# Down projection of a hybrid decoder block: from eight block products to seven

## Chip, core and metric

The kernel runs on one core of a Trainium2 chip. The metric is device time in microseconds (us): the median of several executions of the whole kernel, from launch to the last output byte. Beside it there is one profiled execution, whose trace gives every duration quoted below.

## The reference

One decoder layer on 512 tokens of width 1024, all in float32: a normalised three-branch token mixer with a residual, a normalised convolutional feed-forward part with a residual, and a last RMSNorm. The change touches what follows the up projection:

```python
def conv_ffn(h, w_up, conv_w, conv_b, w_down):          # FFN_DIM = 2816
    up = h @ w_up                                        # 512 x 5632
    up = lax.conv_general_dilated(up, ...) + conv_b      # causal, width 3, per channel
    gate, val = jnp.split(up, 2, axis=-1)
    return (jax.nn.silu(gate) * val) @ w_down            # (512 x 2816) @ (2816 x 1024)
...
    x = x + conv_ffn(rmsnorm(x, norm_ffn), w_up, conv_w, conv_b, w_down)
return rmsnorm(x, norm_final)
```

## The kernel before

**Arithmetic.** A float32 factor is split into a high half (a copy in a TensorE format, `copy_act`, made by ScalarE) and a low half (the value less the high half, made by VectorE). A product is then three matmuls, high x high, high x low and low x high (`mm3m`, L176 to L179). Activations (`gh`, `gl`) are the stationary operand of the down projection, weights (`whi`, `wlo`) the moving one.

**Stages.** After the mixer come the up projection (`up_unit`, 11 chunks c, each with two gate and two value strips of 128 channels), and the down projection (`down_unit`). Each strip of the gated product is `cc[:, 2 + a, :]`, 128 channels x 512 tokens; L1122 and the lines behind it make `gh` and `gl` of it, one stage behind TensorE. The down projection makes four token tiles of 128 in two column halves of 512, each over 22 strips: 4 x 2 x 22 x 3 matmuls of 512 columns. The last tile's last four strips are cut into 256-column pieces (`fin`), so that its result comes in two parts.

**Weights.** A `Chunk` is loaded by one DMA from SyncE's queue into one of two raw buffers of 1 MB (`Chunk.load`, L81), and split piece by piece (`Chunk.split`, L92 is the low half) into the four `whi` and four `wlo` buffers of 128 x 1024.

**Order.** All instructions are written out in a fixed order by `run`: for each unit, first the splits that are due, then functions that `before` or `early` have planned, then the unit's matmuls. Every engine works its own list in that order and waits for semaphores. SyncE's queue is in order too, so a load that waits for a buffer holds up those behind it.

**End.** The residual `x1` stays in SBUF. Each result is added to it by VectorE, squared and summed by ScalarE (L1193), raised to -1/2 by GpSimd (L1211), scaled, and stored by eight DMAs (`finish`).

Of the kernel before, what the change touches and what calls it, by code (L numbers as in the profile page):

```python
# [9 lines left out]
F32 = mybir.dt.float32  # L10
# [8 lines left out]
T = 512  # L19
# [12 lines left out]
def hybrid_block(  # L32
# [19 lines left out]
    def slot(shape, dt=F32, name="s"):  # L52
        return sl.tile(shape, dt, tag="s", name=name)
# [100 lines left out]
    def krows(w, k0, nk, c0, mk=None):  # L154
# [45 lines left out]
    def run(first, live):  # L200
# [9 lines left out]

        def load_to(n):
            while state["loaded"] < min(n, len(order)):
                order[state["loaded"]].load()
# [897 lines left out]
    gh, gl, cc = {}, {}, []  # L1111
    fps = {}

    def up_use(c, a, val):
        ps = fps.pop((c, a, val))
        if not cc:
            cc.append(y8([128, 4, T], name="cc"))
        f = 2 * c + a
        g, v = cc[0][:, a, :], cc[0][:, 2 + a, :]
        if not val:  # L1120
            conv(g, ps, f)
            later.append(lambda: S.activation(g, g, AF.Silu))  # L1122
            return
# [8 lines left out]
        later.append(product)  # L1132

    def up_unit(chunk, c, a, val, o, tag):
        def fn():
# [4 lines left out]
                up_use(c, a, val)  # L1140
        return fn

    gfin = []

    def load_gfin():
        gfin.append(hp_.tile([128, DM], F32, tag="hTh", name="gfin"))
        SY.dma_start(gfin[0], norm_final[None, :].to_broadcast([128, DM]))

    DTAG = (("sc", "sc", "pt", "pt"), ("mm", "mm", "o", "o"))

    def down_unit(chunk, half, k0, n):
        def fn():
            if k0 == 0:
                for t in range(NT):
                    acc[t] = bank(DTAG[half][t], name="acc")
            order = [(t, k) for k in range(n) for t in range(NT)]
            whole = slice(0, 512)
            if k0 + n == NF:
                order = [(t, k) for t in range(NT) for k in range(n)]
                if half == 1:  # L1160
                    order = order[:-n]
            order = [(t, k, whole) for t, k in order]
            final = k0 + n == NF and half == 1
            if final:

                order += [(NT - 1, k, c) for c in (slice(0, 256), slice(256, 512)) for k in range(n)]
                fin = {0: bank("sc", name="fin"), 256: bank("pt", name="fin")}
            for t, k, c in order:
                o = slice(t * 128, t * 128 + 128)
                kk = k0 + k  # L1170
                w = tuple(v[:, c] for v in chunk.get(k))
                if final and t == NT - 1:
                    ps, starts, stops = fin[c.start][:, 0:256], k == 0, k == n - 1
                else:
                    ps = acc[t]
                    starts, stops = kk == 0, kk == (NF - 5 if half == 1 and t == NT - 1 else NF - 1)
                mm3m(ps, gh[kk][:, o], gl[kk][:, o], w, starts, stops)
                if not stops:
                    continue
                if kk < NF - 1:  # L1180
                    y = x1[t // 2][:, t % 2, 512:1024]
                    tt(y, y, ps, ADD)
                    continue
                if half == 0:
                    residual(t, half, acc[t], fss)
                    row = x1[t // 2][:, t % 2, whole]
                    stt(fss[:, 8 + t:9 + t], fss[:, t:t + 1], 1.0 / DM, epsv, MUL, ADD)
                    tt(row, row, gfin[0][:, whole], MUL, G)
                    continue
                y, oc = x1[t // 2][:, t % 2, 512 + c.start:512 + c.stop], cc[0][:, t, c]  # L1190
                ss = fss[:, 4 + t:5 + t] if c.start == 0 else fss[:, 12:13]
                tt(y, y, ps, ADD)
                S.activation(ps, y, AF.Square, accum_out=ss)  # L1193
                for f in rest[:1] if final and t == NT - 1 else rest[:]:
                    rest.remove(f)
                    f()
                tt(oc, y, gfin[0][:, 512 + c.start:512 + c.stop], MUL, G if t < NT - 2 else V)
                parts.append(ss)
                if c.stop == 512:
                    for ss in parts:  # L1200
                        ms = fss[:, 8 + t:9 + t]
                        stt(ms, ss, 1.0 / DM, ms, MUL, ADD)
                    parts.clear()
                    finish(t)
        return fn

    parts, rest = [], []

    def finish(t):
        ms, row, y = fss[:, 8 + t:9 + t], x1[t // 2][:, t % 2, 0:512], cc[0][:, t, :]  # L1210
        G.tensor_tensor(ms, ms, mhalf, op=ALU.pow)  # L1211

        def first():
            copy_act(row, row, scale=ms)
            SY.dma_start(out[0, t * 128:(t + 1) * 128, 0:512], row)

        def second():
            ts(y, y, ms, MUL)
            SY.dma_start(out[0, t * 128:(t + 1) * 128, 512:1024], y)

        rest.extend((first, second))
        if t == NT - 1:
            first()
            second()
        elif t < NT - 2:
            rest.pop(0)()


    for j in range(4):
# [102 lines left out]
                for a in range(2):  # L1332
                    add(ch, up_unit(ch, c, a, val, o, ("mm", "o")[val]))
    u_down = len(units)
    for half in range(2):
        k0 = 0
        for n in (2, 4, 4, 4, 4, 4):
            ch = krows(w_down[0], k0, n, half * 512)
            add(ch, down_unit(ch, half, k0, n))
            k0 += n  # L1340

    def st_(g):
        return lambda: next(g)
# [42 lines left out]
    before(u_down + 1, load_gfin)  # L1386
    run(cu[1], 2)


# [27 lines left out]
```

## Time and profile before

| what | value |
|---|---|
| time, median of 3 runs | 832.47 us (831.61 to 832.5) |
| the profiled execution's own time | 834.41 us |
| its span, first to last instruction | 832.6 us |
| mean granted TensorE clock | 0.989 |
| TensorE matmuls busy | 815.8 us, 98% of the span |
| VectorE, ScalarE, GpSimd busy | 57%, 44%, 19% |
| DMA | 76.60 MB, mean 92 GB/s |

The profiled execution lasted 1.81 us longer than its span, and 1.94 us longer than the median. A matmul's row lasts longer than the step to the next one, since matmuls overlap in the array; what one costs is read from the distance of two starts. In the same way a VectorE or ScalarE row reaches a little into the next one, so distances between starts are used for what a run of instructions takes.

### The profile page before, as it was taken

To read this page: it belongs to the slowest core of one execution; us is meant where nothing else is said; L and a number is where in the kernel's file an instruction comes from. 1 tells how busy PE (TensorE), PEld (TensorE's weight loads), DVE (VectorE), ACT (ScalarE), POOL (GpSimd) and SP (SyncE) were. 2 spreads that over 40 slices of the span, in tenths; PEclk is the share of its full clock that TensorE was granted. 3 is DMA by queue.
4 is the path that set the end of the run, shared out by engine and by line. 5 is a ranking of instruction groups with operands and counts; after the bars stand their busy time and mean duration, and the time that the engine had idled before them with its cause. 6 is when DMAs were issued, how large, how long until landed. Compare 5 with 4: busy or idle time off the path is not lost.

```text
span 832.6 us, 10517 instructions
## 1 busy us (share of the span) xinstructions
PE 815.8 (98%) x4085; PEld 677.2 (81%) x4085; DVE 470.8 (57%) x913; ACT 363.3 (44%) x673; POOL 160.1 (19%) x217
## 2 busy tenths in 40 slices
PE   8999899999999999999999999999999999999996
PEld 7978778778787888888878998888888888888885
DVE  7998666674636638272755466655566555423313
ACT  6446556457354546242443354444444444313212
POOL 6199623523200100032610000000000000002002
PEclk9999799999999999999999999999999999999998
DMA  9332131132331122332261313333333323412402
GB/s 248 96 103 62 40 102 52 51 95 46 63 106 52 53 78 76 102 102 70 93 245 51 99 52 102 101 102 102 101 102 102 101 77 102 167 60 77 152 0 102
DMA packets 68277, 76.60 MB, mean 92 GB/s; under 512 B 8160, under 2 KB 55556, under 8 KB 68228
## 3 DMA queue, kind: packets, MB, share of 16 engines
q1 hardware_dynamic: 67972, 75.89, 28.7%
q8 instruction: 32, 0.52, 0.3%
q0 software_dynamic: 256, 0.05, 0.1%
q14 instruction: 17, 0.14, 0.1%
HBM read 73.81 MB, written 2.12 MB: 91 GB/s over the span
## 4 chain that ended last, share of the span: by engine, by line
PE 84%; DVE 8%; DMA 2%; ACT 2%; issue 1%; POOL 1%; SPq 1%; POOLq 0%; DVEq 0%; ACTq 0%
PE mm L171 10%; PE up L172 10%; PE up L171 10%; PE up L173 10%; PE mm L172 9%; PE mm L173 9%; PE acc L178 6%; PE acc L179 6%; PE acc L177 6%; DVE wlo L92 1%; DVE us L624 1%; PE sc L895 1%; PE sc L763 1%; PE sc L684 1%; PE o L722 1%
## 5 line engine op out<-in xcount | busy, mean ns | idle before, releaser
L92 DVE TENSOR_TENSOR wlo<-raw,whi 128x1024 fp32r<-128x1024 f32 (+1 forms) x126 | 150.3, 1203 | 152.5 <-ACT whi L66 152.4
L66 ACT ACTIVATE whi<-raw 128x1024 fp32r<-128x1024 f32 (+1 forms) x126 | 127.3, 1023 | 58.4 <-PE acc L179 56.2
L171 PE MATMUL up<-hTh,whi 128*128 128x512 f32 (+1 forms) x384 | 142.7, 372 | 0.0
L172 PE MATMUL up<-hTl,whi 128*128 128x512 f32 (+1 forms) x384 | 142.6, 371 | 0.0
L173 PE MATMUL up<-hTh,wlo 128*128 128x512 f32 (+1 forms) x384 | 142.6, 371 | 0.0
L171 PE MATMUL mm<-hTh,whi 128*128 128x512 f32 (+1 forms) x336 | 133.5, 397 | 0.0
L172 PE MATMUL mm<-hTl,whi 128*128 128x512 f32 (+1 forms) x336 | 130.5, 388 | 0.0
L173 PE MATMUL mm<-hTh,wlo 128*128 128x512 f32 (+1 forms) x336 | 130.3, 388 | 0.0
L275 DVE SCALAR_TENSOR_TENSOR cc<-up,cpar,cc 128x511 f32<-128x511 f32 x88 | 65.9, 749 | 97.3 <-ACT cc L1107 95.8
L171 PEld LDWEIGHTS up<-hTh,whi 128*128 128x128 f32 x384 | 72.3, 188 | 12.6
L173 PEld LDWEIGHTS up<-hTh,wlo 128*128 128x128 f32 x384 | 72.3, 188 | 12.5
L172 PEld LDWEIGHTS up<-hTl,whi 128*128 128x128 f32 x384 | 72.3, 188 | 12.3
L171 PEld LDWEIGHTS mm<-hTh,whi 128*128 128x128 f32 x336 | 64.2, 191 | 14.7 <-issue 2.5
L173 PEld LDWEIGHTS mm<-hTh,wlo 128*128 128x128 f32 x336 | 63.9, 190 | 13.1
L172 PEld LDWEIGHTS mm<-hTl,whi 128*128 128x128 f32 x336 | 63.9, 190 | 11.8
L178 PE MATMUL acc<-wlo,gh 128*128 128x512 f32 x172 | 66.9, 389 | 0.0
L179 PE MATMUL acc<-whi,gl 128*128 128x512 f32 x172 | 66.9, 389 | 0.0
L177 PE MATMUL acc<-whi,gh 128*128 128x512 f32 x172 | 66.9, 389 | 0.0
L279 POOL TENSOR_TENSOR x<-x,gfin 128x512 f32<-128x512 f32 x4 | 5.2, 1290 | 296.8 <-ACT acc L1046 296.8
L1107 ACT ACTIVATE cc<-up,cpar 128x512 f32<-128x512 f32 x44 | 34.3, 779 | 61.2 <-PE up L173 60.4
L989 ACT ACTIVATE th<-mm 128x512 f32<-128x512 f32 x24 | 14.3, 595 | 67.3 <-PE mm L173 67.3
L66 ACT ACTIVATE gh<-cc 128x512 fp32r<-128x512 f32 x22 | 13.9, 632 | 59.4 <-DVE cc L279 59.4
(297 smaller groups left out, 1271.4 us busy)
## 6 DMA issues: line engine op xcount, KB each, us to landing
raw<-in_w_up_dram SPq DMA_DIRECT2D x22, 1024.0 KB, 5.1
raw<-in_w_in_dram SPq DMA_DIRECT2D x18, 1024.0 KB, 5.1
raw<-in_w_down_dram SPq DMA_DIRECT2D x10, 1024.0 KB, 5.0
x<-in_x_dram SPq DMA_DIRECT2D x8, 512.0 KB, 6.1
raw<-in_w_in_dram SPq DMA_DIRECT2D x8, 512.0 KB, 5.4
raw<-in_w_out_dram SPq DMA_DIRECT2D x4, 1024.0 KB, 5.0
raw<-in_w_branch_a_dram SPq DMA_DIRECT2D x4, 512.0 KB, 5.9
raw<-in_w_branch_c_dram SPq DMA_DIRECT2D x2, 1024.0 KB, 5.0
```

The lines of the kernel that those rows point to most:

```text
L66: S.activation(o, i, AF.Copy)
L92: (lo_eng or V).tensor_tensor(view(lo), r, view(hi).bitcast(F32), op=ALU.subtract)
L171: PE.matmul(ps, wh, xh, start=first, stop=False)
L172: PE.matmul(ps, wh, xl, start=False, stop=False)
L173: PE.matmul(ps, wl, xh, start=False, stop=last)
L177: PE.matmul(ps, xh, wh, start=first, stop=False)
L178: PE.matmul(ps, xh, wl, start=False, stop=False)
L179: PE.matmul(ps, xl, wh, start=False, stop=last)
L275: emit(lambda: V.scalar_tensor_tensor(o, a, s, b, op0=op0, op1=op1))
L624: V.tensor_copy(US[j][32 * tau:32 * tau + 32], uT[0][32 * j:32 * j + 32].rearrange("p t (c a) -> p t c a", a=4)[:, :, :, tau])
L989: S.activation(t, ps, AF.Tanh, scale=0.5)
L1107: S.activation(dst, ps, AF.Identity, bias=cpar[:, 3, f:f + 1], scale=cpar[:, 2, f:f + 1])
```

## The change

The down projection is done by a one-level Winograd scheme. Tokens, pairs of strips and output columns are each cut in halves, which gives eight block products, and seven products of sums of blocks take their place. A product is 256 tokens x 11 pair rows x 512 columns.

- `sums` forms the token-side sums of a chunk, on VectorE, while the up projection goes on. Operands are (c, 1) to (c, 3) for each chunk c, and (c, 4) for a pair of chunks; each is split into halves by `parts`. Of (c, 1) that happens in `sums`, of (c, 2) for c < 5 too; the other 23 splits are done by `late` at units of the down projection named in a table.
- `Sum` is the weight-side block: up to two pair rows x 512 columns, 512 KB. p1, p2 and p3 use plain blocks. For p5 and p7 a second block is added to the first by an accumulating DMA that GpSimd issues after the plain load has landed. p6 = p5's sum + a block, p4 = p6's sum + a block; these are added by VectorE (L189), as is p5 for the second group of rows.
- The 42 units are in two sweeps: p1, p5, p6, p4 over six groups of pair rows, then p2, p7, p3. One group (`(10, 1)`) has a single row, so its units are half as long.
- `raw_tile`: eight raw homes of 512 KB. Four are the old two raw buffers; the other four (`big`) lie where the up projection's `hTl` was, and are there when its last matmul has read it. A block is split three units ahead of its use; its home's next load is issued then.
- `park` writes `x1` to DRAM during the up projection, `load_x2` reads it back in four pieces of 512 KB in the down projection.
- `ends` adds each finished product to the residual in the order of the scheme, and the last part (`given`, `scaled`) normalises and stores.

```diff
+    class Sum:
...
+        def load(self):
+            self.raw = raw_tile(self.nk)
+            SY.dma_start(self.raw, self.block(self.col, self.row))
+            if self.acc:
+                G.dma_start(self.raw, self.block(*self.acc), accum_op=ADD)
+        def sum(self):
+            if self.plus is not None and not self.acc and not self.summed:
+                V.tensor_tensor(self.raw, self.raw, self.plus.raw, op=ADD)
+            self.summed = True
+        def split(self, i, hi_eng=None, lo_eng=None):
+            r = self.raw
+            self.sum()
+            hi, lo = (piece([128, 2, 512], n)[:, 0:self.nk, :] for n in ("whi", "wlo"))
+            copy_act(hi, r)
+            if self.next is not None and self.next.raw is not None:
+                self.next.sum()
+            V.tensor_tensor(lo, r, hi.bitcast(F32), op=SUB)
...
             if done[ci] == len(c.defs):
-                load_to(ci + 3)
+                load_to(ci + (8 if isinstance(c, Sum) else 3))
...
             tt(v, v, g, MUL)
-            gh[f], gl[f] = slot([128, T], F32R, name="gh"), slot([128, T], F32R, name="gl")
-            copy_act(gh[f], v)
-            later.append(lambda: tt(gl[f], v, gh[f][:, :].bitcast(F32), SUB))
+            if a and c < NP - 1:
+                later.append(lambda: sums(c))
...
+    def parts(key, src, view=lambda t: t):
+        h, l = store(), store()
+        copy_act(view(h), src)
+        tt(view(l), src, view(h).bitcast(F32), SUB)
+        H[key] = (h, l)
+    def sums(c):
...
+        a11, a12, a21, a22 = (v[:, j, t * 256:t * 256 + 256] for t in range(2) for j in range(2))
+        s5 = s6 = a21
+        tt(R[c - c % 2, 4][:, Q1 if c % 2 else Q0], a11, a21, SUB)
+        tt(s5, a21, a22, SUB)
+        parts((c, 1), v[:, 0, :])
+        tt(s6, s5, a11, SUB)
+        if c < FULL:
+            parts((c, 2), v[:, :, Q1], two)
+        else:
+            R[c, 2] = store(F32)
+            copy_act(two(R[c, 2]), v[:, :, Q1])
+        R[c, 3] = store(F32)
+        copy_act(R[c, 3][:, Q0], a12)
+        tt(R[c, 3][:, Q1], a12, s6, ADD)
+    def late(c, i):
+        o = Q0 if (c, i) == (NP - 1, 4) else slice(0, T)
+        parts((c, i), R.pop((c, i))[:, o], lambda t: t[:, o])
...
+    def park():
+        for t in range(NT):
+            SY.dma_start(xd[t * 128:(t + 1) * 128, :], x1[t // 2][:, t % 2, :])
+    def load_x2(t):
+        SY.dma_start(x2[0][:, t, :], xd[t * 128:(t + 1) * 128, :])
+    def raw_tile(nk):
+        j = rn[0] % 8
...
+    def down_unit(blocks, kind, first, last, ts_=(0, 1)):
+        def fn():
+            for t in ts_:
...
+                for i, (ch, k0, k) in enumerate(todo):
+                    xh, xl = (v[:, t * 128:t * 128 + 128] for v in tok(k0 + k, kind))
+                    mm3m(PS[kind, t], xh, xl, ch.get(k), first and i == 0, last and i == len(todo) - 1)
+                if last:
+                    ends(kind, t)
+    def ends(kind, t):
...
+        elif kind == "p3":
+            if t == 1:
+                part(0, 1)
+                power(0)
+            add_to(t, 1, ps)
+            square(t, 1, ps)
+            ys[t] = slot([128, 512], name="y")
+            tt(ys[t], xv(t, 1), gfin[0][:, 512:], MUL)
+            if t == 1:
+                given(0)
+                scaled(3, 0)
+                part(1, 1)
+                power(1)
+                scaled(3, 1)
+                given(1)
...
-    for half in range(2):
-        k0 = 0
-        for n in (2, 4, 4, 4, 4, 4):
...
+    SWEEPS = ((("p1", 0, 0, None), ("p5", 1, 0, "p1"), ("p6", 1, 1, "p5"), ("p4", 0, 1, "p6")),
+              (("p2", 0, 1, None), ("p7", 1, 0, "p3"), ("p3", 1, 1, None)))
+    GROUPS = [(0, 2), (2, 2), (4, 2), (10, 1), (6, 2), (8, 2)]
+    seq = [(kind, g) for g in GROUPS for kind in range(4)]
+    seq2 = [(kind, g) for g in GROUPS[:-2] for kind in range(3)] + [(k, g) for k in (1, 0, 2) for g in GROUPS[-2:]]
...
+            ch.acc = {"p5": (0, 0), "p7": (1, 1)}.get(kind) if (kind, k0) != ("p5", 2) else None
...
+    for u, c, i in ((7, 5, 2), (8, 0, 3), (9, 1, 3), (10, 10, 2), (11, 0, 4), (12, 6, 2), (13, 7, 2), (14, 2, 3),
...
+        before(u_down + u, lambda c=c, i=i: late(c, i))
...
+    before(u_up + 3, park)
+    before(u_down, down_begin)
+    before(u_down + 5, lambda: sums(NP - 1))
+    before(u_down + 23, load_gfin)
+    for t in range(NT):
+        before(u_down + 8 + 2 * t, lambda t=t: load_x2(t))
```

VectorE's list where the up projection ends and the down projection begins (`cc` are the gated strips, `up` their PSUM banks, `wlo` low halves of weights, `raw` and `big` weight homes). Before:

```order
L279 TENSOR_TENSOR cc_4381<-cc_4381 128x512
L275 SCALAR_TENSOR_TENSOR cc_4381<-up_5890,cpar_153,cc_4381 128x511
L275 SCALAR_TENSOR_TENSOR cc_4381<-up_5890,cpar_153,cc_4381 128x510
L92 TENSOR_TENSOR wlo_5919<-raw_5819,whi_5918 128x1024
L92 TENSOR_TENSOR wlo_5923<-raw_5819,whi_5922 128x1024
L279 TENSOR_TENSOR gl_5888<-cc_4381,gh_5887 128x512
L279 TENSOR_TENSOR cc_4381<-cc_4381 128x512
```

Now:

```order
L318 TENSOR_TENSOR cc_4386<-cc_4386 128x512
L314 SCALAR_TENSOR_TENSOR cc_4386<-up_5951,cpar_153,cc_4386 128x511
L314 SCALAR_TENSOR_TENSOR cc_4386<-up_5951,cpar_153,cc_4386 128x510
L189 TENSOR_TENSOR raw_5913<-raw_5913 128x1024
L200 TENSOR_TENSOR wlo_5980<-raw_5913,whi_5979 128x1024
L200 TENSOR_TENSOR wlo_5985<-raw_5913,whi_5984 128x1024
L318 TENSOR_TENSOR cc_4386<-cc_4386 128x512
L189 TENSOR_TENSOR big_5989<-big_5989 128x1024
```

The sum of weight blocks (L189) stands ahead of the low halves and is new; the low half of a strip (`gl`) is gone from here.

VectorE's list around the units with a single row in the first sweep, now (`op` are token-side operands; before there are only low halves of weights in the down projection, L92, and the results):

```order
L200 TENSOR_TENSOR wlo_6181<-big_5989,whi_6180 128x512
L318 TENSOR_TENSOR op_6186<-op_4685,op_6185 128x512
L189 TENSOR_TENSOR big_5989<-big_5989 128x512
L200 TENSOR_TENSOR wlo_6202<-big_5989,whi_6201 128x512
L318 TENSOR_TENSOR op_6208<-ops_5870,op_6207 128x512
L189 TENSOR_TENSOR big_5989<-big_5989 128x512
L200 TENSOR_TENSOR wlo_6225<-big_5989,whi_6224 128x512
```

Each unit there brings a low half, a late split (`op`), and for two of four a sum.

SyncE's queue from the last load of the up projection on, now (a row with x4 stands for four loads; `x2` is the residual):

```order
L81 DMA raw_5719<-in_w_up_dram 128x8x256
L183 DMA raw_5800<-in_w_down_dram 128x2x512 x2
L183 DMA raw_5913<-in_w_down_dram 128x2x512 x2
L183 DMA big_5989<-in_w_down_dram 128x2x512 x4
L183 DMA raw_5800<-in_w_down_dram 128x2x512 x2
L183 DMA raw_5913<-in_w_down_dram 128x2x512 x2
L183 DMA big_5989<-in_w_down_dram 128x512 x4
L183 DMA raw_5800<-in_w_down_dram 128x2x512 x2
L183 DMA raw_5913<-in_w_down_dram 128x2x512
L1254 DMA x2_5988<-xd_154 128x1024
```

Before, twelve loads of a whole raw buffer stood there (the first and the seventh half as large); now 42 of a home, with the four pieces of the residual among them, and on GpSimd's queue eleven accumulating ones.

## Rows read from the trace of the kernel before

**Rows 1.** The page: busy time of the engines, and the chain by engine.
```profile
PE 815.8 (98%) x4085; PEld 677.2 (81%) x4085; DVE 470.8 (57%) x913; ACT 363.3 (44%) x673; POOL 160.1 (19%) x217
...
PE 84%; DVE 8%; DMA 2%; ACT 2%; issue 1%; POOL 1%; SPq 1%; POOLq 0%; DVEq 0%; ACTq 0%
```
**Rows 2.** Windows: stretch, its length, busy us (count) by engine, clock, DMA share, GB/s.
```profile
660.00:700.00 40.00, 40.00 (x178) 33.13 (x177) 23.73 (x30) 17.14 (x22) 0.00 (x0) 1.00 0.31 94
705.95:823.20 117.25, 117.25 (x521) 97.14 (x520) 36.30 (x41) 28.02 (x37) 9.01 (x8) 1.00 0.24 85
```
**Rows 3.** Timeline of TensorE: start, length, engine, line, operation; down projection's first and last.
```profile
705.79 0.39 PE L177 MATMUL acc<-whi,gh 128*128 128x512 f32 x1
706.02 0.39 PE L178 MATMUL acc<-wlo,gh 128*128 128x512 f32 x1
706.24 0.39 PE L179 MATMUL acc<-whi,gl 128*128 128x512 f32 x1
706.47 0.39 PE L177 MATMUL acc<-whi,gh 128*128 128x512 f32 x1
...
822.75 0.28 PE L177 MATMUL fin<-whi,gh 128*128 128x256 f32 x1
...
825.50 0.28 PE L179 MATMUL fin<-whi,gl 128*128 128x256 f32 x1
```
**Rows 4.** Timeline of VectorE and ScalarE around the start of the down projection.
```profile
706.81 1.53 DVE L275 SCALAR_TENSOR_TENSOR cc<-up,cpar,cc 128x511 f32<-128x511 f32 x2 [3.18 <-ACT cc L1107]
708.26 2.35 DVE L92 TENSOR_TENSOR wlo<-raw,whi 128x1024 fp32r<-128x1024 f32 x2
710.52 0.68 DVE L279 TENSOR_TENSOR gl<-cc,gh 128x512 fp32r<-128x512 f32 x1
711.12 0.69 DVE L279 TENSOR_TENSOR cc<-cc 128x512 f32<-128x512 f32 x1
...
706.67 2.00 ACT L66 ACTIVATE whi<-raw 128x1024 fp32r<-128x1024 f32 x2
711.84 0.63 ACT L66 ACTIVATE gh<-cc 128x512 fp32r<-128x512 f32 x1 [3.18 <-DVE cc L279]
```
**Rows 5.** The page: DMA issues, count, KB each, median us to landing; and GpSimd's queue.
```profile
raw<-in_w_down_dram SPq DMA_DIRECT2D x2, 512.0 KB, 3.3
raw<-in_w_down_dram SPq DMA_DIRECT2D x10, 1024.0 KB, 5.0
...
q0 software_dynamic: 256, 0.05, 0.1%
```
**Rows 6.** Windows in which weights, or four 512-KB loads of x, were under way.
```profile
716.00:721.00 5.00, 5.00 (x24) 4.14 (x23) 1.65 (x2) 1.06 (x1) 0.00 (x0) 1.00 0.79 280
...
426.00:428.00 2.00, 2.00 (x10) 1.68 (x9) 0.00 (x0) 0.00 (x0) 0.00 (x0) 1.00 1.06 418
428.00:430.00 2.00, 2.00 (x10) 1.66 (x9) 0.49 (x1) 0.00 (x0) 0.00 (x0) 1.00 1.02 416
```
**Rows 7.** Timeline of GpSimd: a DMA that it issues.
```profile
249.58 0.95 POOL L883 DMA_DIRECT2D d<-nlB  x1 [27.65 <-DVE nlB L879]
```
**Rows 8.** Timeline of the end: VectorE, ScalarE, GpSimd and SyncE's queue.
```profile
825.82 0.42 DVE L279 TENSOR_TENSOR x<-x,fin 128x256 f32<-128x256 f32 x1 [0.33 <-PE fin L179]
826.16 0.48 DVE L269 TENSOR_SCALAR cc<-cc,fss 128x512 f32<-128x512 f32 x1
826.55 0.42 DVE L279 TENSOR_TENSOR cc<-x,gfin 128x256 f32<-128x256 f32 x1
826.89 0.41 DVE L275 SCALAR_TENSOR_TENSOR fss<-fss 128x1 f32<-128x1 f32 x2
...
827.96 0.72 ACT L68 ACTIVATE x<-x,fss 128x512 f32<-128x512 f32 x1 [1.18 <-POOL fss L1211]
...
827.38 0.55 POOL L1211 TENSOR_TENSOR fss<-fss,mhalf 128x1 f32<-128x1 f32 x1 [2.05 <-DVE fss L275]
...
829.14 0.38 SPq L1219 DMA_DIRECT2D out_dram<-cc  x1
```

More of the change, by code (lines that the diff above doesn't have):

```diff
@@ L212, in load_to @@
             while state["loaded"] < min(n, len(order)):
+                if isinstance(order[state["loaded"]], Sum) and rn[0] >= 4 and not RB:
+                    return
                 order[state["loaded"]].load()
@@ L1109, in conv @@
         stt(dst[:, 2:T], ps[:, 0:T - 2], cpar[:, 0, f:f + 1], dst[:, 2:T], MUL, ADD)
-    gh, gl, cc = {}, {}, []
+    cc = []
     fps = {}
@@ L1145, in load_gfin @@
     def load_gfin():
-        gfin.append(hp_.tile([128, DM], F32, tag="hTh", name="gfin"))
+        gfin.append(y8([128, 2 * DM], name="gfin")[:, 0:DM])
         SY.dma_start(gfin[0], norm_final[None, :].to_broadcast([128, DM]))
-    DTAG = (("sc", "sc", "pt", "pt"), ("mm", "mm", "o", "o"))
-    def down_unit(chunk, half, k0, n):
-        def fn():
[L1153 to L1204, printed above, removed]
-        return fn
@@ L1207, in hybrid_block @@
-    parts, rest = [], []
-    def finish(t):
-        ms, row, y = fss[:, 8 + t:9 + t], x1[t // 2][:, t % 2, 0:512], cc[0][:, t, :]
-        G.tensor_tensor(ms, ms, mhalf, op=ALU.pow)
[L1213 to L1226, printed above, removed]
+    def raw_tile(nk):
+        j = rn[0] % 8
+        rn[0] += 1
+        if j < 4 and len(RW) <= j // 2:
+            RW.append(st.tile([128, 2048], F32, tag="raw", bufs=2, name="raw"))
+        t = RW[j // 2][:, j % 2 * 1024:j % 2 * 1024 + 1024] if j < 4 else RB[j - 4]
+        return t.rearrange("p (k n) -> p k n", n=512)[:, 0:nk, :]
@@ new lines, in last_powers, with first_halves, scaled, power @@
+    def last_powers():
+        for t in (2, 3):
+            part(t, 0)
+            part(t, 1)
+            power(t)
+    def first_halves():
+        for t in range(2):
+            part(t, 0)
+            tt(xv(t, 0), xv(t, 0), gfin[0][:, 0:512], MUL)
+    def scaled(t, half):
+        o = slice(half * 512, half * 512 + 512)
+        stt(xv(t, half), xv(t, half), fss[:, 8 + t:9 + t], gfin[0][:, o], MUL, MUL)
+        SY.dma_start(out[0, t * 128:(t + 1) * 128, o], xv(t, half))
+    def power(t):
+        ms = fss[:, 8 + t:9 + t]
+        G.tensor_tensor(ms, ms, mhalf, op=ALU.pow)
@@ L1229, in hybrid_block, with part @@
+    slow = []
+    es = {}
+    def part(t, half):
+        ms, ss = fss[:, 8 + t:9 + t], fss[:, 2 * t + half:2 * t + half + 1]
+        stt(ms, ss, 1.0 / DM, epsv if half == 0 else ms, MUL, ADD)
     for j in range(4):
@@ new lines, in hybrid_block @@
+    seq2 = [(kind, g) for g in GROUPS[:-2] for kind in range(3)] + [(k, g) for k in (1, 0, 2) for g in GROUPS[-2:]]
+    sums_ = []
+    for sweep, order_ in zip(SWEEPS, (seq, seq2)):
+        group = {}
+        seen = []
+        for i, (j, (k0, n)) in enumerate(order_):
+            kind, col, row, plus = sweep[j]
+            ch = group[kind, k0] = Sum(k0, n, col, row)
+            ch.plus = group.get((plus, k0))
+            ch.acc = {"p5": (0, 0), "p7": (1, 1)}.get(kind) if (kind, k0) != ("p5", 2) else None
+            left = sum(sweep[q][0] == kind for q, _ in order_[i + 1:])
+            blocks, tk = [(ch, k0, n)], (0, 1)
+            if kind == "p3" and left < 2:
+                if left:
+                    pair = blocks
+                else:
+                    pair += blocks
+                blocks, tk = pair, (1 - left,)
+            u = add(ch, down_unit(blocks, kind, kind not in seen, left == 0 or len(tk) == 1, tk))
+            seen.append(kind)
+            sums_.append((u, ch))
@@ L1342, in st_ @@
+    before(u_down + 41, lambda: scaled(2, 0), lambda: scaled(2, 1))
+    for d in range(6):
+        before(u_down + 25 + d, lambda: slow.pop(0)())
+    for i, (u, ch) in enumerate(sums_):
+        if i:
+            sums_[i - 1][1].next = ch
+        for d in (2, 3):
+            if i + d < len(sums_):
+                early.setdefault(u, []).append((sums_[i + d][1], 1))
+    early.setdefault(u_down - 1, []).append((sums_[1][1], 1))
     def st_(g):
@@ L1385, in hybrid_block @@
     before(u_up + 2, lambda: norm2(1, ("pt", "sc", "pt", "sc")))
-    before(u_down + 1, load_gfin)
+    before(u_up + 3, park)
[4 more added lines that the diff above has]
+        before(u_down + 8 + 2 * t, lambda t=t: load_x2(t))
     run(cu[1], 2)
```

88 lines of the change are left out of this document (84 added, 4 removed).

## The prediction

> **What bounds the kernel now.** I read the page first: TensorE is busy for 98% of the span and holds 84% of the chain that ended last [rows 1]. Then the windows over the last two stages. In the down projection (705.95 to 823.20) TensorE has no gap, at the full granted clock, while VectorE is busy 36.3 of 117.25 us, ScalarE 28.0, and the DMA engines 24% [rows 2]. So time goes only if matmuls go, and only as long as the others, who get much more to do, keep up. The up projection is no different: no gap, VectorE 23.7 of 40 us [rows 2].
>
> **TensorE's part.** Three matmuls later the start is 0.68 us later (705.79 to 706.47), so one of 512 columns costs 0.227 us; over all 516 of them it is (822.75 - 705.79) / 516 = 0.2267 [rows 3]. The 24 narrow ones run from 822.75 to 825.50 + 0.28. The whole projection takes 825.78 - 705.79 = 119.99 us. The new one has 7 products x 11 pair rows x 2 token tiles x 3 = 462 matmuls of 512 columns, 462 x 0.2267 + 0.17 (the end of the last, whose row is 0.39 long) = 104.9 us. Removed: **15.1 us**, if nothing makes TensorE wait. A full unit of 12 matmuls lasts 2.72 us, one with a single row 1.36; the first sweep 264 x 0.2267 = 59.85 us, the second 44.9.
>
> **VectorE's part.** Steps between starts: 1.13 us for 1024 columns (two from 708.26 to 710.52), 0.60 for 512 (710.52 to 711.12), 0.73 for a fused one (two in 1.45) [rows 4], 0.34 for 256 (826.55 to 826.89) [rows 8]. First sweep:
> low halves of 24 blocks, 20 x 1.13 + 4 x 0.60 = 25.0;
> 13 sums of weight blocks, 11 x 1.13 + 2 x 0.60 = 13.6;
> 13 late splits x 0.60 = 7.8;
> results of p1, p6 and p4, 8 x 0.60 = 4.8;
> what is left of the up projection with the last chunk's sums, 1.45 + 0.60 + 4 x 0.34 + 0.60 = 4.0.
> That is 55.2 of 59.85 us, 92%. The second sweep has 18 low halves (18.8), ten late splits (6.0) and some 14 additions (8.4): 33 of 44.9. The densest place are the four half-length units: in program order they carry 8.65 us of VectorE for 5.44 of TensorE, an excess of 3.2 us. A block is split three units ahead, 8.2 us, so this fits, and I cost VectorE at nothing; its cover is that lead, and a rival below has the price if it is gone. At the start, the block for the third unit is the tight one: conversion ends after 706.81 + 1.45, one sum and one low half at 710.5, needed at 705.79 + 2 x 2.72 = 711.2. ScalarE, at 1.0 us for 1024 columns and 0.63 for 512 [rows 4], has some 33 us in the first sweep and is no question. In the up projection a chunk (four strips, 21.8 us) loses two low halves (1.2) and gets four 256-column sums and one or two low halves (2.0 to 2.6); on 23.7 of 40 us [rows 2] this is hidden behind TensorE. `park` writes 2.1 MB there, where the DMA engines are 31% busy [rows 2]: nothing.
>
> **The DMA part, where the risk is.** Before: 11.5 MB of weights. Now 77 pair-row blocks of 262 KB = 20.2 MB, less four homes (2.1 MB) that are loaded during the up projection, plus 2.1 MB of residual and 0.5 of the norm's weights: 20.7 MB plain in 104.9 us. Weights moved at 280 GB/s with engines 79% busy, which is 354 at full use [rows 6], so this is 58.5 us of engine time. The accumulating DMAs add 20 blocks of 262 KB, 5.2 MB. No row of before shows one. From below: they cost what a plain load does, 14.8 us. From above: GpSimd's queue, the only rows of such issues, moved 0.05 MB in 0.1% of 832.6 us, about 60 GB/s [rows 5], which gives 87 us. These were tiny pieces; the new ones move rows of 2 KB as the plain loads do, so I take the plain load as the nearer row, and count it twice since the home's old content has to be fetched as well: 29.6 us. Sum 88 of 104.9 us. It is not even: in the eighth to fifteenth unit after the start (16.3 us) the ring asks for eight loads, the residual, and three accumulating blocks, 4.2 + 2.1 + 2 x 1.6 = 9.4 MB, 26.6 us at 354 GB/s or 22.5 at the 418 that four 512-KB loads reached [rows 6]: 6 to 10 us over. Against it stands the lead. A home is loaded about ten units ahead and its sum or split begins three to four units ahead, which leaves some 16 us, of which 3.3 go to the load [rows 5], about 0.95 to the issue on GpSimd [rows 7], and 5 to the accumulating transfer at twice the time: 7 left. So waits there between nothing and 3 us; I put **1.0 us**. The unknown's ends are 0 and, from above, 58.5 + 87 - 104.9 = 41 us.
>
> The Trainium skill, "DMA: Bandwidth & Descriptors", section "Rules for kernel authors", speaks against halving the loads: it asks for 1 MiB or more in a transfer. Its fit in "Anatomy of one DMA" (2.0 us and bytes at 436 GB/s) makes 3.2 us of 512 KB, and the row says 3.3. By the rule a ring of half-size loads would be paced by each load's own latency, which is a rival below; the 418 GB/s of four such loads in flight together speak against it here.
>
> **The end.** Before, the last issue of an output stood at 829.14, 3.36 us after the last matmul's end [rows 8]. Now behind the last matmul on VectorE: addition 0.60, scaling 0.60, one more 0.40, a fused one 0.73, the small sum 0.15, about 2.5 us with the start; then GpSimd's power 0.55, ScalarE's scaling 0.72 [rows 8], and the last issues in a queue: 4.3 us. **0.9 us** more.
>
> **Sum.** 832.6 - 15.1 + 0.9 + 1.0 = 819.4 us of span. The profiled execution took 1.81 more than its span and was 1.94 above the median, so the median becomes 832.47 - 13.2 = **819.3 us**. Likeliest case alone: 816 to 822.5.
>
> **Rivals.**
> 1. *The accumulating DMAs are dear, and the DMA engines set the pace.* For: no row bounds them well, and plain traffic alone takes 56% of the stage. Against: rows of 2 KB like the plain ones. With a price of k plain loads the stage needs 58.5 + 14.8 k; it fills 104.9 at k = 3.1, and is slower than before from 58.5 + 14.8 k > 118.1, k = 4.0. At k = 4.5 it is 125.1, 20.2 us of waits, 838.5 us. TensorE waits at p5, p6 and p7 units.
> 2. *VectorE paces the first sweep.* If each of its some 60 instructions costs its whole row (1.22 and 0.69 instead of 1.13 and 0.60, about 9% more, 60.0 us) and 0.1 us for a wait on ScalarE or a load, it needs 66 instead of 59.85 us: 6 us more, 824.5 to 825.5. For: 92% in the sum leaves little. Against: the lead of three units, and light units at both ends of a sweep. Together with short DMA waits this case reaches 829.
> 3. *Each half-size load is paced by its own latency*, the skill's rule: 38 loads x 3.3 us = 125 instead of 104.9, 839 us. Against: seven homes are loading or loaded at a time.
> 4. *Waits just eat the gain*, 13.2 us of them by a mixture of 1 and 2: 832.5.
>
> **Chances.** Forecast 0.57, rival 2 0.25, rival 1 0.12, rival 3 0.02, rival 4 0.04. About 0.2% (1.7 us) is what a measurement of this kernel can tell from no change. Faster by more than that: 0.57 + 0.25 + 0.01 of rival 4 = 0.83; within: 0.03; slower: 0.14. The range from 816 (no waits, no longer end, and 1 us better) to 831 leaves out rivals 1 and 3 and a part of the fourth.
>
> **What would show it.** Right: the first p1 matmul at about 705.8 as before; the down projection's first to last matmul about 105 to 106 us, at a step of 0.227; VectorE busy 85 to 95% in the first sweep, the DMA engines 70 to 85% over both; the last output issued some 4.3 us behind the last matmul. Wrong: gaps on TensorE. If they stand ahead of p5, p6 and p7 units and an accumulating DMA took over 8 us to land, it is rival 1; if the releaser is a low half or a sum on VectorE whose load had landed long before, rival 2; if plain loads land one by one, rival 3. An up projection longer than before by over 1 us would make the cover there wrong.

## The result and the profile after

| | before | after |
|---|---|---|
| time, median (4 runs each) | 832.49 us (831.61 to 832.88) | 819.96 us (819.28 to 820.66) |
| ratio to before, 95% interval | | 0.9851 [0.9834, 0.9868] |
| profiled execution's time, span | 834.41, 832.6 us | 820.41, 818.6 us |
| down projection, first matmul's start to last one's end | 119.99 us | 104.88 us |
| from the last matmul's end to the end of the span | 6.82 us | 9.79 us |

The change makes the kernel 12.5 us faster by the medians. In the two profiles the down projection gave 15.11 us and the end took 2.97 back; a third difference, at the start, is not the change's (below).

The page of the changed kernel, busy time of the engines and the chain by engine; they answer to [rows 1]:

```profile
PE 796.6 (97%) x4007; PEld 660.5 (81%) x4007; DVE 540.5 (66%) x1021; ACT 392.8 (48%) x725; POOL 165.3 (20%) x222
...
PE 80%; POOL 8%; DVE 6%; ACT 2%; issue 2%; DMA 1%; POOLq 0%; SPq 0%; DVEq 0%; ACTq 0%
```

Its timeline of TensorE, the down projection's first matmul, the one three later, and the last [rows 3]:

```profile
703.93 0.39 PE L214 MATMUL p<-whi,op 128*128 128x512 f32 x1
...
704.61 0.39 PE L214 MATMUL p<-whi,op 128*128 128x512 f32 x1
...
808.42 0.39 PE L216 MATMUL p<-whi,op 128*128 128x512 f32 x1
```

All 462 are in the trace and no step between two starts is longer than 0.26 us: TensorE waits for nothing in this stage. Its windows [rows 2]: a stretch of the up projection, the two sweeps, the stretch of 16.3 us for which the prediction saw the DMA engines over-asked, and four stretches of 10.9 us around the change of sweeps, in which they are busiest (columns as there):

```profile
660.00:700.00 40.00, 40.00 (x178) 33.16 (x177) 25.31 (x35) 18.62 (x26) 1.26 (x1) 1.00 0.40 118
703.93:763.80 59.87, 59.87 (x266) 49.61 (x265) 52.43 (x60) 33.69 (x44) 6.86 (x6) 1.00 0.96 300
763.80:808.70 44.90, 44.90 (x199) 36.97 (x197) 36.78 (x55) 24.10 (x39) 5.57 (x6) 1.00 0.59 168
725.70:742.00 16.30, 16.30 (x73) 13.52 (x72) 13.76 (x19) 9.59 (x15) 1.20 (x1) 1.00 0.91 281
742.00:752.90 10.90, 10.90 (x50) 9.02 (x49) 8.56 (x11) 4.79 (x7) 1.20 (x1) 1.00 1.06 348
752.90:763.80 10.90, 10.90 (x50) 9.03 (x49) 10.82 (x12) 7.78 (x10) 2.38 (x2) 1.00 1.02 279
763.80:774.70 10.90, 10.90 (x50) 9.03 (x49) 10.83 (x15) 5.29 (x6) 2.08 (x2) 1.00 1.06 320
774.70:785.60 10.90, 10.90 (x50) 9.04 (x49) 8.90 (x13) 5.25 (x8) 2.38 (x2) 1.00 1.02 266
```

VectorE is busy for 88% of the first sweep (52.43 of 59.87), and from 752.9 to 774.7 almost without a pause (10.82 and 10.83 of 10.90). The DMA engines are full in the first sweep (0.96) and in the first 21.8 us of the second (1.06 and 1.02); over both sweeps they work 59.87 x 0.96 + 44.90 x 0.59 = 84 of 104.8 us, 80%.

The trace's view of the DMAs [rows 5]: the two queues that carry the weights (q0 is GpSimd's, with the accumulating ones; the share is of 16 engines' span), and issues with count, KB each and median us to landing:

```profile
q1 hardware_dynamic: 73828, 88.74, 32.8%
q0 software_dynamic: 2992, 5.29, 3.8%
...
raw<-in_w_down_dram SPq DMA_DIRECT2D x19, 512.0 KB, 8.1
big<-in_w_down_dram SPq DMA_DIRECT2D x16, 512.0 KB, 6.5
...
big<-in_w_down_dram POOLq DMA_DIRECT2D x5, 512.0 KB, 9.0
...
raw<-in_w_down_dram POOLq DMA_DIRECT2D x4, 512.0 KB, 6.0
```

A plain load of 512 KB took 3.3 us to land before and takes 6.5 to 8.1 now, an accumulating one 6.0 to 9.0. The latter's share of the engines is 0.038 x 818.6 = 31.1 us for 5.29 MB, 5.9 us for each MB; all the plain traffic of the kernel has 0.328 x 818.6 = 268.5 us for 88.74 MB, 3.03. So an accumulated byte costs 1.94 plain ones on the whole kernel's average, which holds transfers of many kinds; against the plain weight loads of [rows 6], 354 GB/s at full use or 2.82 us for each MB, it is 2.1. About twice, either way.

The end of the span, VectorE, GpSimd and the last store's issue [rows 8]:

```profile
808.01 0.69 DVE L318 TENSOR_TENSOR y<-x,gfin 128x512 f32<-128x512 f32 x1
808.62 1.41 DVE L314 SCALAR_TENSOR_TENSOR x<-x,fss,gfin 128x512 f32<-128x512 f32 x2
809.94 0.15 DVE L314 SCALAR_TENSOR_TENSOR fss<-fss 128x1 f32<-128x1 f32 x1
810.01 0.68 DVE L318 TENSOR_TENSOR x<-x,p 128x512 f32<-128x512 f32 x1
...
812.46 0.74 DVE L314 SCALAR_TENSOR_TENSOR x<-x,fss,gfin 128x512 f32<-128x512 f32 x1
...
812.62 0.99 POOL L1363 TENSOR_TENSOR fss<-fss,mhalf 128x1 f32<-128x1 f32 x1 [1.90 <-DVE fss L314]
...
814.59 0.41 SPq L1335 DMA_DIRECT2D out_dram<-x  x1
```

The last matmul ends at 808.81. The addition that needs it starts only at 810.01: two fused scalings and a small sum for other token tiles stand ahead of it on VectorE. The last issue is 5.78 us behind the last matmul's end, 3.36 before.

**The start.** The stage begins at 703.93, not at 705.79. A second profile of the kernel before tells why (`e_before_again`): there it began at 704.01. The first matmul of the up projection, in the profile shown above the prediction, in the second profile of the same kernel, and in the changed one:

```profile
463.40 0.28 PE L171 MATMUL up<-hTh,whi 128*128 128x256 f32 x1
...
461.61 0.28 PE L171 MATMUL up<-hTh,whi 128*128 128x256 f32 x1
...
461.54 0.28 PE L208 MATMUL up<-hTh,whi 128*128 128x256 f32 x1
```

From there to the down projection's start it is 242.39 or 242.40 us in all three, so the difference lies ahead of the up projection and is there without the change too. Windows 60 to 100 us, first of the profile shown above the prediction:

```profile
60.00:100.00 40.00, 37.75 (x185) 32.24 (x185) 29.13 (x60) 22.76 (x67) 37.09 (x62) 0.83 0.17 53
```

and of the second profile of the same kernel:

```profile
60.00:100.00 40.00, 35.01 (x197) 29.41 (x197) 29.69 (x60) 22.69 (x67) 37.10 (x62) 0.97 0.16 53
```

The granted clock was 0.83 in one and 0.97 in the other; the changed kernel had 0.98. That varies from run to run. Against the second profile: stage -15.11, end 9.79 - 6.90 = +2.89, start -0.08, together -12.3 of span (830.9 to 818.6), beside -12.5 of the medians.

### The profile page after: what moved, and what is told of

It is laid out like the page before. It is cut to its first block, busy times and chain, and to the rows that moved or that the text cites. A ratio compares the mean times of both kernels' runs of the same rounds, so it can differ in the third digit from the quotient of the medians.

```text
span 818.6 us, 10655 instructions
## 1 busy us (share of the span) xinstructions
PE 796.6 (97%) x4007; PEld 660.5 (81%) x4007; DVE 540.5 (66%) x1021; ACT 392.8 (48%) x725; POOL 165.3 (20%) x222
## 3 DMA queue, kind: packets, MB, share of 16 engines
q1 hardware_dynamic: 73828, 88.74, 32.8%
q0 software_dynamic: 2992, 5.29, 3.8%
## 4 chain that ended last, share of the span: by engine, by line
PE 80%; POOL 8%; DVE 6%; ACT 2%; issue 2%; DMA 1%; POOLq 0%; SPq 0%; DVEq 0%; ACTq 0%
PE up L208 10%; PE up L209 10%; PE up L210 10%; PE mm L208 9%; PE mm L210 9%; PE mm L209 9%; PE p L214 4%; PE p L216 4%; PE p L215 4%; POOL esc L318 1%; POOL vt L318 1%; POOL t L318 1%; PE acc L215 1%; PE acc L216 1%; PE acc L214 1%
## 5 line engine op out<-in xcount | busy, mean ns | idle before, releaser
L92 DVE TENSOR_TENSOR wlo<-raw,whi 128x1024 fp32r<-128x1024 f32 (+1 forms) x104 | 123.0, 1192 | 94.5 <-ACT whi L66 94.4
L210 PEld LDWEIGHTS up<-hTh,wlo 128*128 128x128 f32 x384 | 72.4, 188 | 12.5
L208 PEld LDWEIGHTS up<-hTh,whi 128*128 128x128 f32 x384 | 72.4, 188 | 12.5
L209 PEld LDWEIGHTS up<-hTl,whi 128*128 128x128 f32 x384 | 72.4, 189 | 12.3
L185 POOL DMA_DIRECT2D raw<-in_w_down_dram x5 | 5.7, 1147 | 271.3 <-DVE wlo L92 221.1
L214 PE MATMUL p<-whi,op 128*128 128x512 f32 x146 | 56.9, 389 | 0.0
L216 PE MATMUL p<-whi,op 128*128 128x512 f32 x146 | 56.9, 389 | 0.0
L215 PE MATMUL p<-wlo,op 128*128 128x512 f32 x146 | 56.9, 389 | 0.0
L318 POOL TENSOR_TENSOR th<-th 128x512 f32<-128x512 f32 x15 | 23.8, 1607 | 69.9 <-DVE th L314 69.9
```

Source lines behind the costliest of these rows:

```text
L92: (lo_eng or V).tensor_tensor(view(lo), r, view(hi).bitcast(F32), op=ALU.subtract)
L214: PE.matmul(ps, xh, wh, start=first, stop=False)
L215: PE.matmul(ps, xh, wl, start=False, stop=False)
L216: PE.matmul(ps, xl, wh, start=False, stop=last)
L318: emit(lambda: (eng or V).tensor_tensor(o, a, b, op=op))
```

## The experiments

**e_before_again**: the kernel before once more, one profile. 

> The kernel before, unchanged, for a second profile. If its down projection starts at about 704 us, as in the changed kernel, the 1.9 us between the two profiles ahead of that stage are the granted clock of one stretch (0.83 in one profile, 0.98 in the other, at 60 to 100 us) and no gain of the change. If it starts at 705.8 again, the change moved something earlier.

 Measured 832.64 us, span 830.9; the stage takes 119.99 us again, the end 6.90.

**What is late next.** Four runs, to see how far the covers reach that TensorE hid. Of `e_two`, `e_two_noacc` and `e_acc2` there is one execution each.

`e_two` (one matmul of three left out of the down projection):

```diff
-                    mm3m(PS[kind, t], xh, xl, ch.get(k), ...)
+                    wh, wl = ch.get(k)
+                    PE.matmul(PS[kind, t], xh, wh, ...)
+                    PE.matmul(PS[kind, t], xh, wl, ...)
```

> Leaves out the third matmul (low x high) of every product of the down projection; loads, sums, splits and additions stay. TensorE then needs 308 x 0.2267 = 69.8 us for it instead of 104.9, so its length shows what the others need. Theory (TensorE paces, VectorE is next with 89 us of work, the DMA engines third with 84): 89 to 96 us, total time 804 to 812. Rival 1 (the DMA engines, 96% busy in the first sweep, already set the pace): no shorter than 103 us, total 818 or more. If neither is near: 70 us, total 785.

 Measured 819.76 us: with a third of its matmuls gone (308 x 0.2267 = 69.8 us of work) the stage still takes 101.18 us, between the theory's 96 and the rival's 103, so neither held. The waits of ScalarE in the stage (who waited for whom, us in total, times, longest):

```profile
ACT whi L66 <- DMA big<-in_w_down_dram: 22.4, 5, 6.9
```

The conversions wait for loads; VectorE, which I had expected to be next, is busy 85.6 of these 101.2 us, the DMA engines 84%.

`e_two_noacc` (the same, and the accumulating DMAs left out):

```diff
-            if self.acc:
-                G.dma_start(self.raw, self.block(*self.acc), accum_op=ADD)
```

> The same, and the eleven accumulating DMAs are left out as well (31 us of DMA engine time). If VectorE sets the pace of the run with two matmuls, this one is as long, within 2 us. If the DMA engines do, it is 10 us shorter or more.

 Measured 807.6 us, stage 87.08: 12.2 us shorter than `e_two`, so the accumulating DMAs made that one late. Its windows over the stage:

```profile
703.00:763.00 60.00, 51.44 (x201) 37.31 (x200) 57.56 (x69) 37.41 (x49) 0.00 (x0) 0.97 0.82 286
763.00:790.00 27.00, 25.98 (x111) 20.17 (x110) 26.84 (x36) 16.43 (x25) 0.00 (x0) 1.00 0.43 133
```

Now VectorE has no time left (57.56 of 60, 26.84 of 27). So three times stand behind each other in this stage: TensorE 104.9, the loads with their accumulating DMAs about 101, VectorE about 87. Whether the engines' own time or the landing of one transfer behind the other makes the 101 was not told apart. Those 101 hold some matmuls at the lower clock, so the DMAs' own floor may lie a little below.

`e_noacc` (the accumulating DMAs alone left out). 

> The eleven accumulating DMAs are left out (p5 and p7 take the plain block), nothing else. Theory (they are hidden): the same time within 1 us, ratio to the changed kernel 0.999 to 1.001, the DMA engines' share in the first sweep down from 0.96 to about 0.75. Rival 1: 3 us shorter or more.

 Measured 820.51 us (820.33 to 820.66), ratio 0.9856 [0.9837, 0.9876]; stage 104.88, no wait. The DMA engines' share in the first sweep fell from 0.96 to 0.80. The accumulating DMAs are fully hidden, as the theory had it.

`e_acc2` (each issued twice):

```diff
                 G.dma_start(self.raw, self.block(*self.acc), accum_op=ADD)
+                G.dma_start(self.raw, self.block(*self.acc), accum_op=ADD)
```

> Every accumulating DMA is issued twice (its block is added twice). DMA engine time goes from 84 to 115 us, against 104.9 of TensorE. Theory (hidden by a margin of some 10 us and by the lead of the ring): waits of 15 to 30 us on TensorE, total 835 to 850. If accumulating DMAs are cheap and far from the bound: under 3 us, total below 823. If each is paced by its own latency of some 9 us, one after the other: 11 x 9 = 99 us less what the lead hides, total over 860.

 Measured 857.7 us, above the 835 to 850 of the theory and short of the 860 of the third case; stage 142.60, 37.7 us of it waits and slower steps. GpSimd's queue, and what TensorE waited for:

```profile
q0 software_dynamic: 5728, 10.54, 7.3%
```

```profile
PE p L215 <- ACT whi L66: 21.5, 6, 8.3
```

The queue's share is 0.073 x 855.9 = 62.5 us, 31.4 more, for 5.25 MB more: the price seen in the changed kernel again. The stage grew by more than that, 37.7 us, and the DMA engines are only 80% busy over it. The second accumulate must wait for the first to land (POOL waited 48.9 us in six waits for `big` alone), so a block passes three latencies in a row; and the clock falls behind long waits (below). How much each has of the excess was not told apart.

**The parts of the change that keep the covers.**

`e_accfirst` (the first sums not on VectorE; a twelfth accumulating DMA for p5's second group):

```diff
-            ch.acc = {"p5": (0, 0), "p7": (1, 1)}.get(kind) if (kind, k0) != ("p5", 2) else None
+            ch.acc = {"p5": (0, 0), "p7": (1, 1)}.get(kind)
```

> Undoes the first sums on VectorE: p5's block for the second group of rows gets its sum by an accumulating DMA like the other groups, so there are twelve. Its home is free only when the up projection has ended, and it is wanted by the sixth unit, 13.6 us later. Theory (a chain of load, about 8 us, and accumulating transfer, about 9, does not fit into that): waits of 3 to 7 us before the p5, p6 and p4 units of that group, total 823 to 827. Rival (the lead of three units covers it): under 1 us.

 Measured 827.75 us (826.83 to 828.36), ratio 0.9943 [0.9928, 0.9958]: more than half of the gain is gone. Timeline of TensorE (idle time before and its releaser in brackets) and the GpSimd issue:

```profile
717.76 0.39 PE L216 MATMUL p<-whi,op 128*128 128x512 f32 x1
720.58 0.80 PE L214 MATMUL p<-whi,op 128*128 128x512 f32 x1 [2.44 <-ACT whi L66]
721.84 0.80 PE L215 MATMUL p<-wlo,op 128*128 128x512 f32 x1 [0.46 <-DVE wlo L200]
722.43 0.63 PE L216 MATMUL p<-whi,op 128*128 128x512 f32 x1
722.86 0.63 PE L214 MATMUL p<-whi,op 128*128 128x512 f32 x1
...
727.71 0.40 PE L214 MATMUL p<-whi,op 128*128 128x512 f32 x1
...
709.67 1.20 POOL L185 DMA_DIRECT2D big<-in_w_down_dram  x1 [21.96 <-DMA big<-in_w_down_dram]
```

The accumulating DMA is issued at 709.67 and the conversion that waits for it starts at 719.47, 9.8 us later; the block is late by one wait. That wait is not the whole price. Behind it matmuls follow each other at 0.427 us instead of 0.227, the granted clock is 0.50 (720.5 to 726.5), that is 1.2 of 2.4 GHz. Steps longer than 0.26 us sum to 6.3 us over the usual: 4.0 in the first three, the waits with the slow steps in them, and 2.3 in twelve slow steps behind. The stage is 6.36 us longer, within the 3 to 7 expected.

`e_ring6` (six homes instead of eight):

```diff
-        j = rn[0] % 8
+        j = rn[0] % 6
...
-                load_to(ci + (8 if isinstance(c, Sum) else 3))
+                load_to(ci + (6 if isinstance(c, Sum) else 3))
```

> Six homes instead of eight. A load is issued two units later, so some five units (13.6 us) are left for a plain load and the accumulating DMA behind it, 8 + 9 us in the changed kernel. Theory (DMA time needs the depth): waits at most p5 and p7 units, 10 to 40 us in all, total 830 to 860. Rival (with fewer transfers in flight each lands sooner, 3.3 + 5 us): under 3 us.

 Measured 827.85 us (826.66 to 830.81), ratio 0.9948 [0.9929, 0.9967]; stage 111.89, +7.0. More than the rival's 3, less than the 10 I had as lower end. The picture is that of `e_accfirst`: one wait at 743.83 (2.7 us over the usual step), then eight slow steps in a row, and a second wait at 800.21, 1.0 us. Six homes hold enough lead for all but two places.

`e_lump` (the late splits of the token operands up to three in a unit, just ahead of the unit that needs them, instead of one a unit and earlier; the beginning of the table of 23):

```diff
-    for u, c, i in ((7, 5, 2), (8, 0, 3), (9, 1, 3), (10, 10, 2), (11, 0, 4), ...
+    for u, c, i in ((9, 5, 2), (13, 10, 2), (17, 6, 2), (17, 7, 2), (21, 8, 2), ...
```

> Undoes the spreading of the conversions: each late split stands in the unit just ahead of the one that needs it, up to three in one unit, instead of one per unit over the whole stage. Theory (VectorE and ScalarE are full on average near the change of sweeps, so a lump stands in the way of the low halves there): waits of 2 to 6 us between the 20th and the 30th unit. Rival (the lead covers lumps): under 1 us.

 Measured 826.63 us (825.26 to 827.81), ratio 0.9935 [0.9918, 0.9952]; stage 110.47, +5.6. VectorE there, and TensorE at the same place:

```profile
757.98 1.22 DVE L200 TENSOR_TENSOR wlo<-raw,whi 128x1024 fp32r<-128x1024 f32 x1
759.12 0.69 DVE L318 TENSOR_TENSOR op<-op 128x512 fp32r<-128x512 f32 x1
759.72 0.69 DVE L318 TENSOR_TENSOR op<-ops,op 128x512 fp32r<-128x512 f32 x1
```

```profile
758.54 0.39 PE L215 MATMUL p<-wlo,op 128*128 128x512 f32 x1
759.86 0.50 PE L216 MATMUL p<-whi,op 128*128 128x512 f32 x1 [0.93 <-DVE op L318]
```

Two splits in one unit come behind the low half of a weight block, and TensorE has to wait for the split. Six such waits of 0.5 to 1.1 us, with short steps behind them, sum to 5.3 us; the clock stays at 1.00 here. They lie between 737 and 797 us, not between the 20th and the 30th unit alone (753 to 780 in the changed kernel). VectorE's work over the stage is the same as in the changed kernel (89.1 and 89.3 us busy). The table heaps the splits up and moves them nearer to their use; which of the two costs more was not told apart.

`e_vsums` (all sums of p5 on VectorE, accumulating DMAs for p7 alone):

```diff
-            ch.acc = {"p5": (0, 0), "p7": (1, 1)}.get(kind) if (kind, k0) != ("p5", 2) else None
+            ch.acc = {"p7": (1, 1)}.get(kind)
```

> All of p5's sums on VectorE, so five more additions there (5.1 us) and six accumulating DMAs instead of eleven (13 us of DMA engine time less). VectorE has then about 58 of 59.9 us in the first sweep. Theory (TensorE paces; VectorE has 6 to 7 us to spare in the first sweep and the three-unit lead evens it out): within 1.5 us of the changed kernel. Rival 2 (VectorE paces the first sweep as soon as it is full): 4 us or more.

 Measured 820.49 us (819.27 to 820.85), ratio 0.9854 [0.9839, 0.9869]; stage 104.88. Its first sweep:

```profile
704.00:763.87 59.87, 59.87 (x266) 49.58 (x265) 57.10 (x67) 34.01 (x44) 2.67 (x3) 1.00 0.84 277
```

Five more sums on the engine that I held to be at 92%, which is now busy 57.10 of 59.87 us, and no wait: rival 2 is refuted with room left.

`e_x2once` (the four pieces of the residual fetched at one unit):

```diff
-        before(u_down + 8 + 2 * t, lambda t=t: load_x2(t))
+        before(u_down + 8, lambda t=t: load_x2(t))
```

> The four pieces of the residual are loaded one behind the other at the ninth unit instead of at four units; 2.1 MB stand ahead of the next weight blocks. Theory (TensorE has the DMA's margin of some 4 us left and the ring's lead): waits of 0 to 2 us. Rival (no margin, since the DMA engines are full): 4 us or more, about the time of three more pieces.

 Measured 821.98 us (820.62 to 823.21), ratio 0.9877 [0.9863, 0.9891]; stage 105.65: three longer steps at 756 to 760, 0.8 us. Fetching it in pieces is worth that.

**The end.**

`e_tail` (end reordered, and two multiplications by the norm's weights given to GpSimd):

```diff
-            tt(xv(t, 0), xv(t, 0), gfin[0][:, 0:512], MUL)
+            tt(xv(t, 0), xv(t, 0), gfin[0][:, 0:512], MUL, G)
...
-    before(u_down + 40, first_halves)
-    before(u_down + 41, lambda: scaled(2, 0), lambda: scaled(2, 1))
+    before(u_down + 40, lambda: scaled(2, 0), lambda: scaled(2, 1), first_halves)
```

and in p3's end the scalings of tile 3 behind those that the last tile needs. 

> The end alone: the two scalings of the third token tile stand ahead of the last additions instead of between them, the norm's weights are multiplied onto the first two tiles by GpSimd, and the small sum that the last power needs stands ahead of the last fused scalings. Theory (the end, 9.8 us from the last matmul, is VectorE's queue: its last addition started 1.2 us after the last matmul had ended): 1.5 to 2.2 us less than the changed kernel. Rival (the end is the outputs' stores): under 0.5 us.

 Measured 821.6 us (820.13 to 823.41), ratio 0.9874 [0.9858, 0.9890]; the end took 10.60 us instead of 9.79. The expectation failed. VectorE and GpSimd there:

```profile
806.07 2.44 DVE L314 SCALAR_TENSOR_TENSOR x<-x,fss,gfin 128x512 f32<-128x512 f32 x2
808.44 1.30 DVE L314 SCALAR_TENSOR_TENSOR fss<-fss,epsv 128x1 f32<-128x1 f32 x2
...
806.39 3.26 POOL L318 TENSOR_TENSOR x<-x,gfin 128x512 f32<-128x512 f32 x2 [0.81 <-ACT p L1279]
```

While GpSimd multiplies, two fused scalings take 2.44 us (1.41 in the changed kernel) and two sums of one column 1.30 (0.15 each). The Trainium skill, "SBUF — State Buffer", section "Who interferes with whom", says that a VectorE instruction with two SBUF inputs contends with a GpSimd instruction that reads SBUF; all of these have two, and the trace agrees, with 2.0 us lost.

`e_end` (the same aim, nothing on GpSimd): the additions of p7 ahead of one weight split, their squares as a block behind them, and the fused scalings put where VectorE had waited:

```diff
                 given(0)
-                scaled(3, 0)
                 part(1, 1)
                 power(1)
+                given(1)
                 scaled(3, 1)
-                given(1)
...
+    def last_squares():
+        for t in (2, 3):
             square(t, 0, PS["p7", t - 2])
             square(t, 1, PS["p7", t - 2])
...
+    aux_more.append(u_down + 38)
...
-    before(u_down + 39, last_powers)
-    before(u_down + 40, first_halves)
-    before(u_down + 41, lambda: scaled(2, 0), lambda: scaled(2, 1))
+    before(u_down + 39, last_squares, last_powers, lambda: scaled(2, 0))
+    before(u_down + 40, lambda: scaled(2, 1), first_halves)
+    before(u_down + 41, lambda: scaled(3, 0))
```

> The changed kernel with the last instructions of VectorE and ScalarE in another order, nothing given to GpSimd: the four additions of p7 ahead of one weight split, their squares behind them as a block, the fused scalings of the third and fourth token tile spread into the places where VectorE waited for squares, one of them left to the very end. No operation is added or removed. Theory (the 9.8 us behind the last matmul are VectorE's queue: the last addition starts 1.2 us after the last matmul's end because scalings stand ahead of it, and 1.5 us of waits for squares come earlier): TensorE's part stays at 104.88 us, the stretch from the last matmul's end to the end of the span falls from 9.8 to 7.5 to 8.2 us, the time by 1.6 to 2.3 us, ratio to the kernel before about 0.983. Rival (the stores and their queue set the end, the order of the arithmetic does not): that stretch stays within 0.5 us of 9.8, no change. If the split that now stands behind the additions comes late, TensorE's part grows instead, by up to 1 us.

 Measured 818.46 us (818.31 to 820.48, 5 runs), ratio 0.9834 [0.9819, 0.9849]; stage 104.88, end 8.0 us instead of 9.79. VectorE, GpSimd's last power and the last issue:

```profile
808.71 0.15 DVE L315 SCALAR_TENSOR_TENSOR fss<-fss 128x1 f32<-128x1 f32 x1
809.43 0.69 DVE L319 TENSOR_TENSOR x<-x,p 128x512 f32<-128x512 f32 x1 [0.57 <-PE p L216]
...
811.38 0.55 POOL L1366 TENSOR_TENSOR fss<-fss,mhalf 128x1 f32<-128x1 f32 x1 [1.90 <-DVE fss L315]
...
812.37 0.75 DVE L315 SCALAR_TENSOR_TENSOR x<-x,fss,gfin 128x512 f32<-128x512 f32 x1
...
813.41 0.41 SPq L1362 DMA_DIRECT2D out_dram<-x  x1
```

The last addition now waits for TensorE and no longer for VectorE's own queue (matmul's end 809.39, start 809.43). The last issue is 4.02 us behind the matmul's end. The theory held in the profile, 1.8 us of the end; by the medians it is 1.5 us better than the changed kernel, just under the 1.6 expected, but the two intervals overlap, so the times alone don't settle that.

## Why the prediction was right

**TensorE, -15.1 predicted, -15.11 measured.** 462 equal steps, no wait. Counting matmuls was enough, because all covers held.

**VectorE, predicted 0, measured 0.** It was busy 88% of the first sweep where my sum said 92%: five of the eight result additions and one sum of weight blocks that I counted lie outside these 59.87 us. Rival 2 asked whether a lead of three units absorbs the dense places. It does, even with five more sums (`e_vsums`), but not if the late splits are heaped up (`e_lump`, +5.6 us). So the mean load does not decide; how the splits are spread and how early they stand does. In the up projection VectorE went from 23.7 to 25.3 of 40 us, which TensorE hid as forecast; it is no longer than before (242.39 us, the start, above).

**DMA, predicted +1.0, measured 0.** The price that no row showed was taken as twice a plain load, 29.6 us in all; the queue's row gives 31.1, about twice per byte of such loads. My sum was 88 us of engine time, the windows say 84: one of the eleven accumulating DMAs is issued at 685.99, before the stage. The place of 6 to 10 us over was put at 725.7 to 742.0; there the engines are at 0.91 and move 4.6 MB (281 GB/s) of the 9.4 that I had asked of them, and the rest comes later, with the engines full to 785.6. The lead of eight homes absorbs that (with six, +7.0). A limit like rival 1's is close: with TensorE's work cut the stage ends at about 101, some 3.7 below TensorE's 104.9. But its formula (58.5 + 14.8 k) does not give what a dearer accumulation costs: `e_acc2`, k = 4 by engine time, should wait 13 us and the stage grew by 37.7, with the engines 80% busy. The rival's break-even has a slip besides: 118.1 leaves out the 1.0 us of waits that stands in the forecast already, so it should be 119.1 (k = 4.1). I had said that an accumulating DMA of over 8 us with gaps would show the rival; it took 9.0 to land, and there were no gaps, since the time to land is hidden by the lead.

**Rival 3 (each half-size load paced by its latency)** fell: plain loads take 6.5 to 8.1 us to land, twice as long as my 3.3, and TensorE doesn't notice, as several are under way at a time. The Trainium skill ("DMA: Bandwidth & Descriptors", "Rules for kernel authors") names at least 1 MiB per DMA for the most bandwidth; here 512-KB loads keep the engines at 1.06 and 348 GB/s (742.00 to 752.90). That each such load would be paced by its own latency was my reading of that rule and does not stand in it. The page's fit that I set beside the 3.3 us is given there for DMAs that GpSimd issues; the 3.3 us are of loads of SyncE's queue.

**The end, predicted +0.9, measured +2.9.** This is the term that was mis-sized. I counted the chain that hangs on the last matmul as if VectorE were free when it ends. It was not: work for other token tiles stood ahead of it, 1.2 us of delay (808.81 to 810.01). From there to the start of GpSimd's power it is 2.61 us, near the 2.5 of my sum, fused scaling included. The power took 0.99 us instead of the 0.55 that I used: a second fused scaling (812.46) runs beside it on VectorE. In `e_end` that scaling comes later, VectorE runs nothing beside the power, and it takes 0.55. From the last issue to the end of the span it is 4.0 us instead of 3.46, which I did not take apart. The errors of +1.0 for waits and -2.0 for the end have opposite signs: that the sum of -13.2 came so near to -12.5 is luck in part.

## What to carry to other kernels

Where an engine has no gap, the gain of fewer instructions is their count times the step; the work goes into asking whether each cover holds at its densest place, and spread and lead (homes of a ring, how early a split stands) decide that, not the mean load. At the end of a kernel, write down each engine's whole queue from the last result on, with what is left over from earlier tiles, and not only the chain that hangs on that result. A wait on TensorE of a few us can cost its own length again (`e_accfirst`: 2.9 us of waits, 6.36 us of stage).

## What the runs showed of the hardware that was not expected

- The clock behind a wait: behind the steps that grew by 2.6 and 2.7 us (`e_accfirst`, `e_ring6`) came eleven and seven at 0.427 us (granted clock 0.50 from 720.5 to 726.5 in the first); behind those that grew by 0.5 to 1.1 us in `e_lump` and `e_x2once` came none.
- An accumulating DMA costs about twice the engine time of plain bytes (5.9 us for each MB, against 3.03 on the kernel's average and 2.82 in [rows 6]), and 6.0 (`raw`) to 9.0 us (`big`) to land for 512 KB; its issue holds GpSimd for 0.9 to 1.3 us.
- A GpSimd multiplication of 512 columns beside VectorE made fused scalings there 1.7 times as long (2.44 instead of 1.41 us for two). The other way round, one fused scaling on VectorE beside GpSimd's power of one column went with 0.99 us for it instead of 0.55 (changed kernel and `e_tail` against `e_end`).
